# Clearing two mask rows by a transfer instead of two POOL memsets, and folding one small VectorE maximum into the instruction before it, in a streaming attention and recurrence layer

## Chip, cores and metric

The kernel runs on one core of a Trainium2 chip. The metric is the device time of one execution in microseconds (us); the times shown are medians over runs. One execution was also taken with the hardware profiler, and all rows below come from it.

The engines are named as in the profile: PE is TensorE (PEld its weight loads), DVE is VectorE, ACT is ScalarE, POOL is GpSimd, SP is the engine that issues most transfers.

## What is computed

One encoder layer is applied to a prompt of 1024 frames and to 64 frames that continue another stream (256 cached frames). Two branches share one input projection: eight softmax heads of width 64 whose logits carry a cumulative log-forget bias ("FoX"), and four gated linear-recurrence heads ("HGRN2"). Cut to the part that the change touches:

```python
def fox_attend(q, k, v, c_q, c_k, q_pos, k_pos):
    s = jnp.einsum('bqhd,bkhd->bhqk', q, k) * (FOX_HEAD_DIM ** -0.5)
    s = s + (jnp.swapaxes(c_q, 1, 2)[..., :, None] - jnp.swapaxes(c_k, 1, 2)[..., None, :])
    mask = k_pos[None, :] <= q_pos[:, None]
    s = jnp.where(mask, s, -jnp.inf)
    p = jax.nn.softmax(s, axis=-1)
    return jnp.einsum('bhqk,bkhd->bqhd', p, v)
```

The softmax needs, for each query, the maximum of its logits over all earlier keys.

## The kernel before

The kernel first computes the value columns of the prompt (until about 60 us), then the attention (about 60 to 345 us), then the recurrence and the output projection. In the attention the eight heads are taken pair by pair (`PAIRS = (1, 2, 3, 0)`, half `s` 0 and then 1 of each pair). Head n attends while head n+1 is prepared, and projections of later stages (line 234, and 217 for one of them) are laid between as fill work for PE. A generator writes this order by hand, and the tile framework's scheduler then orders the instructions of each engine, by program order and by when it takes operands to be ready; so an edit can also exchange neighbours on an engine.

Per half `s` there is one buffer of each operand: `KX[s]`, `KY[s]` (keys), `QX[s]`, `QY[s]` (queries), all with 128 partitions. In `QY[1]` partitions 64 to 127 hold the queries and partitions 0 to 3 hold rows for the bias and the maximum: rows 0 and 1 are ones, rows 2 and 3 later receive the negated maximum of each query in two parts. The maxima are themselves found by matmuls that read `QY[1]` whole (`Y0[1]` is partitions 0 to 127), so rows 2 and 3 must be zero then, and must be cleared after the head before has used them.

The preparation of a head, in the order of `prepare`:

- `k_prep` copies and splits the keys (ACT line 706, POOL line 711, a transfer at line 710);
- `q_prep` does the same for the queries (ACT line 737, POOL line 743), and for `s = 1` it clears the rows (lines 734 and 735, POOL);
- `max_prep(s, c)` finds the maxima for queries 0 to 511 (`c = 0`) and 512 to 1023 (`c = 1`), four tiles of 128 queries each. PE line 775 makes the logits of one tile in a PSUM bank; for keys on the diagonal piece DVE line 777 adds the mask and takes the maximum in one custom instruction (followed by a small read of its accumulator), and for `c = 1` the earlier 512 keys are first reduced by DVE line 780 into columns 4 to 7 of `mx`. DVE line 783 joins the two;
- `max_columns` makes the two parts of the negated maximum in `mxs` (DVE lines 749 and 750, four columns), and `put_rows` transposes them with four small matmuls (PE line 758) into a PSUM bank, from which ACT line 760 puts them into `QY`;
- `sample_max` does the same for the 64 continued frames (DVE lines 792, 793, 749, 750 with one column, and one more matmul at line 758).

The attention proper is `scores` (PE lines 819 and 820, DVE line 822 for the mask, ACT lines 825 and 826, DVE line 827) and `values` (PE line 844).

Of the kernel before, what the change touches and what calls it, by code (L numbers as in the profile page):

```python
# [13 lines left out]
ALU = mybir.AluOpType  # L14
# [6 lines left out]
T = SEQ + DEC  # L21
# [7 lines left out]
NEG = -3.0e38  # L29
# [32 lines left out]
def f32(ap):  # L62
    return ap.bitcast(F32)
# [3 lines left out]
def tile_fox_hgrn2(  # L67
# [7 lines left out]
    act, dve, pool, pe, sync = nc.scalar, nc.vector, nc.gpsimd, nc.tensor, nc.sync  # L75
# [7 lines left out]
    def nm(s):  # L83
        cnt[0] += 1
        return f"{s}_{cnt[0]}"
# [4 lines left out]
    def bank(tag):  # L90
        return ps.tile([P, 512], F32, tag=tag, name=nm(tag), bufs=PSB[tag])
# [293 lines left out]
    with tc.tile_pool(name="start", bufs=2, side="right") as sp:  # L385
# [132 lines left out]
        def aqt(shape, dt, name):  # L518
            return aq.tile(shape, dt, tag=name, name=name)
# [8 lines left out]
        KY = [aqt([P, KW], F32R, f"KY{s}") for s in range(2)]  # L528
        QY = [aqt([P, T], F32R, f"QY{s}") for s in range(2)]
# [100 lines left out]
    with actx:  # L630
# [66 lines left out]
        def halves(s):  # L697
            return slice(64 * s, 64 * s + 64), slice(64 - 64 * s, 128 - 64 * s)
# [31 lines left out]
        def q_prep(p_, s, c, first):  # L730
            r, o = halves(s)
            qT = qTs[p_]
            if c == 0 and s and p_ != PAIRS[0]:
                pool.memset(f32(QY[s][0:4, :]), 0.0)
                pool.memset(f32(QY[s][0:2, :]), 1.0)
            cs = (slice(0, 512), slice(512, T))[c]
            act.activation(QY[s][r, cs], qT[r, cs], AF.Copy)
            yield 0.0
            if first:
                act.activation(QX[s][o, cs], qT[r, cs], AF.Copy)  # L740
            else:
                sync.dma_start(f32(QX[s][o, cs]), f32(QY[s][r, cs]))
            pool.tensor_tensor(QX[s][r, cs], qT[r, cs], f32(QY[s][r, cs]), op=ALU.subtract)
            yield 0.0

        def max_columns(c, mx, tiles, rows):

            ms = mxs[c]
            dve.tensor_scalar(ms[:rows, :tiles, 2], mx, -1.0, None, op0=ALU.mult)
            dve.scalar_tensor_tensor(ms[:rows, :tiles, 3], mx, -1.0, f32(ms[:rows, :tiles, 2]), op0=ALU.mult,  # L750
                                     op1=ALU.subtract)
# [11 lines left out]
        def max_prep(s, c):  # L763

            qy, ky = QY[s], KY[s]
            rows = Y0[s]
            mx = a2.tile([P, 8], F32, tag="mx", name=nm("mx"))
            for piece in range(c + 1):
                for i in range(4):
                    qs = slice(c * 512 + i * P, c * 512 + (i + 1) * P)  # L770
                    k0 = piece * 512
                    diag = piece == c
                    n = (i + 1) * P if diag else 512
                    pb = bank("tp")
                    pe.matmul(pb[:, :n], qy[rows, qs], ky[rows, k0:k0 + n], start=True, stop=True)  # L775
                    if diag:
                        dve.tensor_tensor_reduce(pb[:, :n], pb[:, :n], cmask[:, 512 - n:512], 1.0,  # L777
                                                 NEG, ALU.add, ALU.max, mx[:, i:i + 1])
                    else:
                        dve.tensor_reduce(mx[:, 4 + i:5 + i], pb[:, :n], axis=AX.X, op=ALU.max)  # L780
                    if diag and i == 3:
                        if c:
                            dve.tensor_tensor(mx[:, 0:4], mx[:, 0:4], mx[:, 4:8], op=ALU.max)
                        max_columns(c, mx[:, 0:4], 4, P)
                    yield max(n / 2.4, 107)

# [10 lines left out]
        def prepare(p_, s, first=False):  # L797

            rest = max_prep(s, 1)
            steps = [k_prep(p_, s, first), q_prep(p_, s, 0, first), max_prep(s, 0), q_prep(p_, s, 1, first), islice(rest, 2),  # L800
                     put_rows(0, s, 4, P), rest, sample_max(s), put_rows(1, s, 4, P), put_rows(2, s, 1, DEC)]
            if first:
                steps[4:6] = steps[5:3:-1]
            steps.insert(1 if first else 8, v_prep(p_, s))
            for g in steps:
                for x in g:
                    yield x
# [690 lines left out]
    for i, rows, src in tok_tiles[:SAMPLE_POS] + tok_tiles[NT:] + tok_tiles[SAMPLE_POS:NT]:  # L1498
# [3 lines left out]
        mx = fin.tile([P, 2, 8, P], F32R, tag="mx", name=nm("mx"))  # L1502
# [102 lines left out]
```

## Time and profile before

| | us |
|---|---|
| median of 3 runs (lowest to highest) | 721.27 (721.17 to 721.51) |
| the profiled execution, its own time | 721.17 |
| its span, first to last instruction | 719.4 |
| PE busy | 702.7 (98% of the span) |
| DVE, ACT, POOL busy | 454.1, 343.5, 192.1 |

A busy PE is the bound on average, but an average hides single stalls; the rows below are read from the stretches where PE stood still. Times in the rows are from the span's start, and the profiled execution took 1.8 us more than its span.

### The profile page before, as it was taken

The page shows a single profiled execution, that of the slowest core. Times are in us where ns is not written, and L with a number is a line of the kernel's source. Part 1 is how long each engine was busy: PE and PEld are TensorE (multiplying, and loading weights), DVE is VectorE, ACT ScalarE, POOL GpSimd, SP SyncE. Part 2 cuts the span into 40 slices and gives each one's busy share as a digit, 9 for nine tenths or more (in the row PEclk, how much of TensorE's full clock was granted, in tenths as well). Part 3 has the DMA queues.
Part 4 walks back from the last instruction along what each step waited for, and adds up shares of the span by engine and source line. Part 5 has one row for each costly group of instructions (what it writes and reads, how often), then busy time and mean ns, then how long its engine had stood idle before and what let it go on. Part 6 is the DMA issues. An engine that isn't in the chain of part 4 may idle for free.

```text
span 719.4 us, 11880 instructions
## 1 busy us (share of the span) xinstructions
PE 702.7 (98%) x4319; PEld 634.7 (88%) x4319; DVE 454.1 (63%) x1145; ACT 343.5 (48%) x877; POOL 192.1 (27%) x252
## 2 busy tenths in 40 slices
PE   9999999999999998999999999999999999999995
PEld 7889989899888897898999999999999998888885
DVE  4445267666777666775536967765795689763541
ACT  6755454657557475867562324224222333323542
POOL 4044932545246234524310001000100100012422
PEclk9999999999999999999999999999999999999999
DMA  8823321221122012110312101002100104331211
GB/s 313 328 84 96 96 99 29 57 81 47 32 92 56 15 28 81 39 30 4 131 44 59 30 31 40 3 30 67 34 31 30 38 34 138 131 111 58 89 44 60
DMA packets 23451, 51.00 MB, mean 71 GB/s; under 512 B 5616, under 2 KB 8512, under 8 KB 23392
## 3 DMA queue, kind: packets, MB, share of 16 engines
q1 hardware_dynamic: 23216, 50.15, 21.8%
q8 instruction: 34, 0.56, 0.3%
q14 instruction: 25, 0.20, 0.1%
q10 hardware_dynamic: 176, 0.09, 0.1%
HBM read 36.32 MB, written 9.56 MB: 64 GB/s over the span
## 4 chain that ended last, share of the span: by engine, by line
PE 87%; DVE 6%; ACT 4%; issue 1%; DMA 0%; POOLq 0%; DVEq 0%; SPq 0%; POOL 0%; ACTq 0%
PE pj L234 36%; PE pj L1384 13%; PE pj L217 6%; PE av L844 6%; PE st L819 2%; PE tp L775 2%; PE st L820 2%; PE pj L440 2%; PE tp L440 2%; PE av L440 2%; PE st L440 2%; PE st L1192 1%; PE st L1271 1%; PE pj L211 1%; PE pj L1378 1%
## 5 line engine op out<-in xcount | busy, mean ns | idle before, releaser
L234 PE MATMUL pj<-hT,whi 128*128 128x364 f32 (+1 forms) x1152 | 213.1, 332 | 0.0
L234 PEld LDWEIGHTS pj<-hT,whi 128*128 128x128 f32 x1152 | 193.3, 189 | 4.6 <-issue 0.3
L234 PE MATMUL pj<-hT,wlo 128*128 128x364 f32 (+1 forms) x576 | 110.0, 331 | 0.0
L234 PEld LDWEIGHTS pj<-hT,wlo 128*128 128x128 f32 x576 | 97.5, 188 | 3.1 <-issue 0.3
L827 DVE TENSOR_TENSOR pl<-st,ph 128x512 fp32r<-128x512 f32 (+1 forms) x96 | 53.1, 556 | 39.2 <-ACT st L826 36.9
L825 ACT ACTIVATE ph<-st 128x512 fp32r<-128x512 f32 (+1 forms) x96 | 46.8, 488 | 60.4 <-DVE st L822 39.1
L107 POOL TENSOR_SCALAR rr<-ss 128x4 f32<-128x4 f32 (+1 forms) x12 | 2.3, 194 | 250.8 <-ACT og L1306 250.6
L1384 PE MATMUL pj<-hT,mx 128*128 128x512 f32 (+1 forms) x264 | 56.3, 374 | 0.0
L1384 PEld LDWEIGHTS pj<-hT,mx 128*128 128x128 f32 x264 | 46.3, 188 | 9.9
L170 ACT ACTIVATE whi<-wr 128x256 fp32r<-128x256 f32 (+1 forms) x112 | 38.6, 407 | 33.8 <-PE pj L234 18.8
L171 POOL TENSOR_TENSOR wlo<-wr,whi 128x256 fp32r<-128x256 f32 (+1 forms) x56 | 39.8, 738 | 39.8 <-ACT whi L170 23.1
L826 ACT ACTIVATE st<-st 128x512 f32<-128x512 f32 (+1 forms) x96 | 46.5, 485 | 0.0
L819 PE MATMUL st<-QX,KX 128*128 128x512 f32 (+1 forms) x96 | 35.5, 370 | 3.4 <-DVE pl L827 3.3
L217 PE MATMUL pj<-whi,hT 128*128 128x264 f32 (+1 forms) x256 | 37.0, 287 | 0.0
L1384 PE MATMUL pj<-hT,mxp 128*128 128x512 f32 x144 | 36.4, 403 | 0.0
L777 DVE CUSTOM_DVE_ANT_0 tp<-tp,cmask 128x128 f32<-128x128 f32 (+1 forms) x64 | 31.1, 501 | 7.3 <-PE tp L775 6.9
L217 PEld LDWEIGHTS pj<-whi,hT 128*128 128x128 f32 x256 | 33.9, 189 | 1.7 <-issue 0.3
L711 POOL TENSOR_TENSOR KX<-kT,KX 64x544 fp32r<-64x544 f32 x16 | 21.6, 1354 | 50.9 <-ACT KX L706 42.3
L844 PE MATMUL av<-ph,VH 128*128 128x512 f32 (+1 forms) x96 | 34.8, 363 | 0.2 <-ACT ph L825 0.2
L820 PE MATMUL st<-QY,KY 68*128 68x512 f32 (+3 forms) x96 | 33.5, 348 | 0.0
L844 PE MATMUL av<-pl,VH 128*128 128x512 f32 (+1 forms) x96 | 33.2, 346 | 0.0
L844 PE MATMUL av<-ph,VL 128*64 128x512 f32 (+1 forms) x96 | 32.4, 338 | 0.0
(311 smaller groups left out, 1358.4 us busy)
## 6 DMA issues: line engine op xcount, KB each, us to landing
wr<-in_w_t_dram SPq DMA_DIRECT2D x24, 512.0 KB
x<-in_xT_dram SPq DMA_DIRECT2D x16, 272.0 KB
xn<-in_x_prompt_dram SPq DMA_DIRECT2D x8, 512.0 KB
wo_raw<-in_w_out_dram SPq DMA_DIRECT2D x8, 512.0 KB
yp<-in_x_prompt_dram SPq DMA_DIRECT2D x6, 512.0 KB
out_dram<-yp SPq DMA_DIRECT2D x12, 256.0 KB
out_dram<-kT SPq DMA_DIRECT2D x4, 544.0 KB
wv<-in_w_v_dram SPq DMA_DIRECT2D x8, 256.0 KB
```

Source lines behind the costliest of these rows:

```text
L170: act.activation(hf[:, cs], raw[:, cs], AF.Copy)
L171: self.eng.tensor_tensor(lf[:, cs], raw[:, cs], f32(hf[:, cs]), op=ALU.subtract)
L217: pe.matmul(pb[:rows, :width], a[:, j, t0:t0 + rows], w[j // 4][b][:, j % 4, :], start=(g == 0 and j == 0), stop=(g == 2 and j == 7))
L234: pe.matmul(pb[:, :n], w[:, j, :], h[:, j, t0:t0 + n], start=(g == 0 and j == 0), stop=(g == 2 and j == 7))
L440: pe.matmul(pb[:, :WV], x[:, j, t0:t0 + P], w[:, j, :], start=(j == 0 and a == 0 and b == 0), stop=(j == 7 and a == 1))
L819: pe.matmul(st[:, :n], kx[:, ks], qx[:, qs], start=True, stop=False)
L820: pe.matmul(st[:, :n], ky[YM[s], ks], qy[YM[s], qs], start=False, stop=True)
L825: act.activation(ph[:, :n], st[:, :n], AF.Exp)
L826: act.activation(st[:, :n], st[:, :n], AF.Exp)
L827: dve.tensor_tensor(pl[:, :n], st[:, :n], f32(ph[:, :n]), op=ALU.subtract)
L844: pe.matmul(av[mm, cols], w[:, b, :], x[:, :n], start=(b == 0 and w is VH[s] and x is ph), stop=(b == nblk - 1 and w is VL[s]), skip_group ...
L1384: pe.matmul(pb[:rows, :n], mx[:, a, j, :rows], wo[b][:, j0 + j, c0:c0 + n], start=(g == 0 and j == 0), stop=(g == 2 and j == nj - 1))
```

## The change

```diff
@@ q_prep
             if c == 0 and s and p_ != PAIRS[0]:
-                pool.memset(f32(QY[s][0:4, :]), 0.0)
-                pool.memset(f32(QY[s][0:2, :]), 1.0)
+
+                sync.dma_start(f32(QY[s][2:4, :]), f32(KY[s][4:6, 0:T]))
@@ max_prep
                     if diag:
                         dve.tensor_tensor_reduce(pb[:, :n], pb[:, :n], cmask[:, 512 - n:512], 1.0,
-                                                 NEG, ALU.add, ALU.max, mx[:, i:i + 1])
+                                                 mx[:, 4 + i:5 + i] if c else NEG, ALU.add, ALU.max,
+                                                 mx[:, i:i + 1])
                     else:
                         dve.tensor_reduce(mx[:, 4 + i:5 + i], pb[:, :n], axis=AX.X, op=ALU.max)
                     if diag and i == 3:
-                        if c:
-                            dve.tensor_tensor(mx[:, 0:4], mx[:, 0:4], mx[:, 4:8], op=ALU.max)
                         max_columns(c, mx[:, 0:4], 4, P)
```

Three times in the program (the preparation of the fourth, sixth and eighth head) two POOL memsets of 4 and 2 partitions x 1088 give way to one transfer of 2 partitions x 1088 on SP's queue, from two partitions of `KY[1]` that hold zeros throughout. Eight times the DVE instruction of line 783 goes, and in exchange 32 of the 64 custom maxima (line 777 with `c = 1`) start from a column of `mx` instead of a constant. In the rows of the changed kernel lines 779 and 780 count one more, and lines from 784 on one less.

The engines' orders differ otherwise in a few places. The first is the end of the seventh head's maxima (in the program: the last rows of `max_prep(0, 1)` and `sample_max(0)` of pair 0). On DVE there stood before (names with numbers are single buffers; `mxs_547` is the four-column result, `mxs_548` the one-column result):

```order
L827 TENSOR_TENSOR pl_3244<-st_3239,ph_3243 128x256
L783 TENSOR_TENSOR mx_3105<-mx_3105 128x4
L792 TENSOR_TENSOR tp_3277<-tp_3277,cmask 64x64
L749 TENSOR_SCALAR mxs_547<-mx_3105 128x4
L822 TENSOR_TENSOR st_3283<-st_3283,kmask 128x128
L750 SCALAR_TENSOR_TENSOR mxs_547<-mx_3105,mxs_547 128x4
L793 TENSOR_REDUCE mx_3276<-tp_3277 64x1
L822 TENSOR_TENSOR st_3298<-st_3298,kmask 128x128
L749 TENSOR_SCALAR mxs_548<-mx_3276 64x1
L750 SCALAR_TENSOR_TENSOR mxs_548<-mx_3276,mxs_548 64x1
```

and now, on the same engine and at the same place:

```order
L826 TENSOR_TENSOR pl_3236<-st_3231,ph_3235 128x256
L749 TENSOR_SCALAR mxs_547<-mx_3097 128x4
L791 TENSOR_TENSOR tp_3268<-tp_3268,cmask 64x64
L750 SCALAR_TENSOR_TENSOR mxs_547<-mx_3097,mxs_547 128x4
L821 TENSOR_TENSOR st_3274<-st_3274,kmask 128x128
L792 TENSOR_REDUCE mx_3267<-tp_3268 64x1
L821 TENSOR_TENSOR st_3289<-st_3289,kmask 128x128
L749 TENSOR_SCALAR mxs_548<-mx_3267 64x1
L750 SCALAR_TENSOR_TENSOR mxs_548<-mx_3267,mxs_548 64x1
```

Line 783 is gone, and one mask (822, now 821) has moved from between lines 749 and 750 to behind them. On POOL at that place the eighth head's preparation and a weight split (line 171) stood before as:

```order
L171 TENSOR_TENSOR wlo_3265<-wr_2559,whi_3264 128x256 x4
L727 TENSOR_TENSOR VL_680<-vnat_91,VH_544 128x512
L734 MEMSET QY_543 4x1088
L711 TENSOR_TENSOR KX_677<-kT_1988,KX_677 64x544
L735 MEMSET QY_543 2x1088
L171 TENSOR_TENSOR wlo_3372<-wr_3274,whi_3371 128x256
```

and now:

```order
L171 TENSOR_TENSOR wlo_3256<-wr_2553,whi_3255 128x256 x4
L727 TENSOR_TENSOR VL_680<-vnat_91,VH_544 128x512
L711 TENSOR_TENSOR KX_677<-kT_1984,KX_677 64x544
L171 TENSOR_TENSOR wlo_3362<-wr_3265,whi_3361 128x256
L852 TENSOR_TENSOR mixF_2505<-mixF_2505,rd_3329 64x512
```

The key split of line 711 now follows line 727 directly. On PE the same place read before:

```order
L844 MATMUL av_3101<-ph_3243,VH_545 128x256
L234 MATMUL pj_3362<-hT,whi_3264 128x364
L819 MATMUL st_3298<-QX_678,KX_676 128x512
L820 MATMUL st_3298<-QY_542,KY_540 128x512
L844 MATMUL av_3101<-pl_3244,VH_545 128x256
L758 MATMUL tp_3311<-ident,mxs_547 4x128 x4
L844 MATMUL av_3101<-ph_3243,VL_681 64x256
L758 MATMUL tp_3320<-ident,mxs_548 4x64
L234 MATMUL pj_3362<-hT,whi_3264 128x364 x6
```

and now:

```order
L843 MATMUL av_3093<-ph_3235,VH_545 128x256
L234 MATMUL pj_3352<-hT,whi_3255 128x364 x2
L818 MATMUL st_3289<-QX_678,KX_676 128x512
L819 MATMUL st_3289<-QY_542,KY_540 128x512
L758 MATMUL tp_3302<-ident,mxs_547 4x128 x4
L843 MATMUL av_3093<-pl_3236,VH_545 128x256
L843 MATMUL av_3093<-ph_3235,VL_681 64x256
L758 MATMUL tp_3311<-ident,mxs_548 4x64
L234 MATMUL pj_3352<-hT,whi_3255 128x364 x5
```

One projection matmul (234) has moved ahead of the four transposing matmuls of line 758, and one of line 844 behind them. The second place is the end of the first head's maxima. DVE there read before:

```order
L777 ISA tp_1038,mx_980<-tp_1038,cmask 128x512
L777 ISA mx_980 128x1
L792 TENSOR_TENSOR tp_1057<-tp_1057,cmask 64x64
L783 TENSOR_TENSOR mx_980<-mx_980 128x4
L822 TENSOR_TENSOR st_1069<-st_1069,kmask 128x128
L749 TENSOR_SCALAR mxs_547<-mx_980 128x4
L793 TENSOR_REDUCE mx_1056<-tp_1057 64x1
L750 SCALAR_TENSOR_TENSOR mxs_547<-mx_980,mxs_547 128x4
L827 TENSOR_TENSOR pl_1074<-st_1069,ph_1073 128x128
L749 TENSOR_SCALAR mxs_548<-mx_1056 64x1
L750 SCALAR_TENSOR_TENSOR mxs_548<-mx_1056,mxs_548 64x1
```

and now:

```order
L777 ISA tp_1038,mx_980<-tp_1038,cmask,mx_980 128x512
L777 ISA mx_980 128x1
L791 TENSOR_TENSOR tp_1056<-tp_1056,cmask 64x64
L826 TENSOR_TENSOR pl_1034<-st_1029,ph_1033 128x256
L749 TENSOR_SCALAR mxs_547<-mx_980 128x4
L792 TENSOR_REDUCE mx_1055<-tp_1056 64x1
L750 SCALAR_TENSOR_TENSOR mxs_547<-mx_980,mxs_547 128x4
L821 TENSOR_TENSOR st_1068<-st_1068,kmask 128x128
L749 TENSOR_SCALAR mxs_548<-mx_1055 64x1
L750 SCALAR_TENSOR_TENSOR mxs_548<-mx_1055,mxs_548 64x1
L826 TENSOR_TENSOR pl_1073<-st_1068,ph_1072 128x128
```

The one-column results (749 and 750 into `mxs_548`) now stand ahead of the subtraction (827, now 826) that they stood behind.

## Rows read from the trace of the kernel before

**Rows 1.** The profile's page: busy time, share of the span and number of instructions of two engines, and the chain that ended last by engine.
```profile
PE 702.7 (98%) x4319; PEld 634.7 (88%) x4319; DVE 454.1 (63%) x1145; ACT 343.5 (48%) x877; POOL 192.1 (27%) x252
PE 87%; DVE 6%; ACT 4%; issue 1%; DMA 0%; POOLq 0%; DVEq 0%; SPq 0%; POOL 0%; ACTq 0%
```

**Rows 2.** PE's own waits over the whole span: who waited for whom, us in total, times, longest.
```profile
PE st L819 <- DVE pl L827: 3.3, 5, 1.0
PE tp L758 <- DVE mxs L750: 3.3, 3, 2.4
```

**Rows 3.** Busy time by stretch, PE alone. Columns: stretch, its length, PE busy us (instructions), granted clock (1.00 is 2.4 GHz), busy share of the DMA engines, GB/s.
```profile
282.10:285.50 3.40, 0.65 (x7) 1.00 0.56 196
285.50:288.92 3.42, 3.42 (x15) 0.58 0.00 0
288.92:292.33 3.41, 3.41 (x21) 0.92 0.00 0
```

**Rows 4.** Timeline of PE around 284 us. Columns, here and in the timelines below: start us, us, engine, line, operation, out<-in, form, count, and in brackets the idle time before it and what ended it.
```profile
281.82 0.28 PE L844 MATMUL av<-pl,VH 128*128 128x256 f32 x1
284.52 0.40 PE L758 MATMUL tp<-ident,mxs 128*4 128x128 f32 x4 [2.42 <-DVE mxs L750]
...
285.37 0.19 PE L758 MATMUL tp<-ident,mxs 64*4 64x64 f32 x1 [0.33 <-DVE mxs L750]
...
285.49 1.73 PE L234 MATMUL pj<-hT,whi 128*128 128x364 f32 x6
...
294.15 1.50 PE L234 MATMUL pj<-hT,whi 128*128 128x364 f32 x8
```

**Rows 5.** Timeline of DVE in the same stretch.
```profile
281.11 1.01 DVE L783 TENSOR_TENSOR mx<-mx 128x4 f32<-128x4 f32 x1
...
282.18 0.89 DVE L749 TENSOR_SCALAR mxs<-mx 128x4 fp32r<-128x4 f32 x1
282.24 1.01 DVE L822 TENSOR_TENSOR st<-st,kmask 128x128 f32<-128x128 f32 x1
283.17 1.29 DVE L750 SCALAR_TENSOR_TENSOR mxs<-mx,mxs 128x4 fp32r<-128x4 f32 x1
284.39 0.47 DVE L793 TENSOR_REDUCE mx<-tp 64x1 f32<-64x320 f32 x1
284.79 0.28 DVE L822 TENSOR_TENSOR st<-st,kmask 128x128 f32<-128x128 f32 x1
...
285.16 0.15 DVE L750 SCALAR_TENSOR_TENSOR mxs<-mx,mxs 64x1 fp32r<-64x1 f32 x1
```

**Rows 6.** Timeline of POOL in the same stretch; POOL's next instruction after these is at 290.87.
```profile
280.80 1.29 POOL L727 TENSOR_TENSOR VL<-vnat,VH 128x512 fp32r<-128x512 f32 x1
282.05 0.99 POOL L734 MEMSET QY<- 4x1088 f32 x1
283.12 1.32 POOL L711 TENSOR_TENSOR KX<-kT,KX 64x544 fp32r<-64x544 f32 x1
284.38 0.99 POOL L735 MEMSET QY<- 2x1088 f32 x1
```

**Rows 7.** Timeline of DVE in the preparation of the fourth head: the same instructions, first with POOL idle and then, at 188.86, with POOL's line 711 running from 188.62 to 189.97.
```profile
187.13 0.15 DVE L783 TENSOR_TENSOR mx<-mx 128x4 f32<-128x4 f32 x1
187.32 0.17 DVE L749 TENSOR_SCALAR mxs<-mx 128x4 fp32r<-128x4 f32 x1
187.53 0.17 DVE L750 SCALAR_TENSOR_TENSOR mxs<-mx,mxs 128x4 fp32r<-128x4 f32 x1
...
188.86 1.12 DVE L750 SCALAR_TENSOR_TENSOR mxs<-mx,mxs 64x1 fp32r<-64x1 f32 x1
```

**Rows 8.** Groups of DVE instructions by form: count | busy us, mean ns of one | idle before. Line 974 scales a PSUM tile by one value per partition, line 822 adds two tiles.
```profile
L822 DVE TENSOR_TENSOR st<-st,kmask 128x128 f32<-128x128 f32 x64 | 19.8, 310 | 8.4 <-PE st L820 8.3
L974 DVE TENSOR_SCALAR hi<-pj,rn 128x128 f32<-128x128 f32 x16 | 5.5, 344 | 7.1 <-ACT hi L973 6.9
L777 DVE CUSTOM_DVE_ANT_0 tp<-tp,cmask 128x128 f32<-128x128 f32 x16 | 4.7, 293 | 1.9 <-PE tp L775 1.9
```

**Rows 9.** Timelines of DVE and PE at the end of the first head's maxima.
```profile
99.56 0.29 DVE L827 TENSOR_TENSOR pl<-st,ph 128x128 fp32r<-128x128 f32 x1 [0.56 <-ACT st L826]
...
99.93 0.15 DVE L750 SCALAR_TENSOR_TENSOR mxs<-mx,mxs 64x1 fp32r<-64x1 f32 x1
...
100.14 0.19 PE L758 MATMUL tp<-ident,mxs 64*4 64x64 f32 x1 [0.51 <-DVE mxs L750]
```

**Rows 10.** Timelines of DVE, POOL and PE at the end of the second head's maxima.
```profile
124.54 1.01 DVE L750 SCALAR_TENSOR_TENSOR mxs<-mx,mxs 128x4 fp32r<-128x4 f32 x1
...
124.17 1.36 POOL L711 TENSOR_TENSOR KX<-kT,KX 64x544 fp32r<-64x544 f32 x1 [4.41 <-ACT KX L706]
...
129.53 0.39 PE L819 MATMUL st<-QX,KX 128*128 128x256 f32 x1 [1.04 <-DVE pl L827]
```

**Rows 11.** Timelines of ACT, SP and PE: the copy that line 711 waits for, the weight transfer issued just ahead of where the new transfer is to stand, and the first matmuls that read the cleared rows.
```profile
280.70 0.66 ACT L706 ACTIVATE KX<-kT 64x544 fp32r<-64x544 f32 x1
...
280.87 0.35 SPq L160 DMA_DIRECT2D wr<-in_w_t_dram  x1
...
289.22 0.52 PE L775 MATMUL tp<-KY,QY 128*128 128x128 f32 x2
```

**Rows 12.** Timeline of PE in the preparation of the sixth head, at full clock, a little behind that head's transposes.
```profile
224.70 0.39 PE L819 MATMUL st<-QX,KX 128*128 128x256 f32 x1 [0.75 <-DVE pl L827]
```

## Prediction

> **What bounds the kernel.** I read the page first: PE is busy 98% of the span and carries 87% of the chain that ended last [rows 1]. An edit that takes work from DVE and POOL (63% and 27% busy) can therefore give back only time in which PE stood still or ran slowly. Next come PE's own waits, which are short [rows 2]: the longest two kinds are 3.3 us each, and the one that the change touches is line 758 (the transposes of the maxima) waiting for line 750. Of its 3.3 us, 2.4 are a single wait. So I went to that wait, in the timelines around 284 us.
>
> There PE finishes the subtraction part of line 844 at 282.1 and starts line 758 only at 284.52; 0.33 us more are lost before the one-column transpose at 285.37 [rows 4]. In the stretch 282.10 to 285.50 PE is busy 0.65 of 3.40 us, and behind it the granted clock is 0.58 and then 0.92 of full, which between two levels (1.00 for 2.4 GHz, 0.5 for 1.2 GHz) means some 3.4 us at 1.2 GHz [rows 3]. So the stall costs twice: 2.75 us of standing still, and after it (1 - 0.58) x 3.42 + (1 - 0.92) x 3.41 = 1.7 us of lost clock.
>
> Why was line 750 late? DVE's three small instructions 783, 749 and 750 took 1.01, 0.89 and 1.29 us [rows 5], where the same ones take 0.15, 0.17 and 0.17 with POOL idle [rows 7]. Each ended within 0.04 us of the end of a POOL instruction: 783 at 282.12 (POOL's 727 ends at 282.09), 749 at 283.07 (the memset 734 ends at 283.04), 750 at 284.46 (711 ends at 284.44) [rows 5, 6]. The same happens at 188.86, where line 750 runs to 189.98 and POOL's 711 to 189.97 [rows 7]. So one DVE instruction was held behind one POOL instruction, three times in turn, and the change takes away one of each: 783 on DVE and 734 on POOL.
>
> **The rule behind it.** These rows show small SBUF-to-SBUF instructions of DVE waiting out a whole POOL instruction. The Trainium skill's page "SBUF — State Buffer" (SBUF: two separate sides) says the same: VectorE and GpSimd arbitrate for a port pair, "an exclusive lock, not a bandwidth split", held for the whole instruction by whichever starts first. The trace agrees with the holding. What would follow if DVE were the one to start first is the third case below.
>
> **Term 1, the stall at 284 us.** Without the memset, line 711 follows 727 at 282.09; its operand is ready, since line 706 ends at 281.36 [rows 6, 11]. It takes 1.32 us, to 283.41. Line 749 now stands where 783 stood, is held by 727 and ends at 282.12; line 750 comes behind it and is held by 711, to 283.44. Line 758 followed 750's end by 0.06 us, so it starts at 283.50 instead of 284.52. From 750's end to the one-column transpose passed 0.91 us (284.46 to 285.37); now one more mask lies in it (line 822, 0.28 us long, of which I count 0.20 since DVE's instructions overlap a little [rows 5]), so that transpose starts at 283.44 + 0.91 + 0.20 = 284.55, 0.82 us earlier than 285.37. One projection matmul now lies ahead of the wait instead of behind it: about 0.17 us (1.50 us for eight with a last end of some 0.33, [rows 4]). Together 1.0 us. Bounds: 0 if 750 is held as long as before by something else, 1.8 us in the third case.
>
> **Term 2, the clock.** What PE stands still there shrinks from 2.75 to about 1.9 us, in two pieces (to 283.50, then about 0.55 us). Does the clock still fall? The rows that bound it: the stall of 2.42 and 0.33 us was followed by a fall [rows 3, 4]; the one of 1.04 us at 129.53 was not, nor 0.75 at 224.70 [rows 10, 12] (the only stretch at low clock inside the kernel's work is the one of rows 3). The new value lies between. I take "no fall" as likelier, because the idle time is cut by a third and broken up. The gain is then at most 1.7 us; at full clock ACT and DVE have less time ahead of PE, and at the sibling place PE waits 0.75 us for line 827 [rows 12], so at least 0.95. I take 1.5.
>
> **Term 3, the first head.** There the one-column transpose waits 0.51 us for line 750, which stands behind a subtraction (827) that itself waits 0.56 us for ACT [rows 9]. The new order puts 749 and 750 ahead of that subtraction. I take 0.4 us, bounds 0.5 gained and 0.3 lost (the order also moves one mask of line 822 behind other work there, and ACT's exponentials with it, by about that).
>
> **Term 4, the second head.** With 783 gone and 750 moved ahead of the reduction 793, line 750 is due about 0.4 us earlier than 124.54, that is at about 124.15. POOL's 711, which held it for 1.01 us, starts at 124.17 [rows 10]. Who is first is open. If 750 is, the DVE work behind it moves up by some 0.7 us, and of the 1.04 us that PE waits at 129.53 up to 0.4 goes. I take 0, with 0.4 as bound.
>
> **Term 5, the new operand.** 32 maxima now read a start value per partition. The trace has no such form of line 777; the nearest rows: a PSUM tile of 128x128 scaled by one value per partition takes 344 ns, two tiles added take 310, and the maximum itself 293 [rows 8]. So 0 to 51 ns each, 0 to 1.6 us over DVE in all, against 8 x 0.15 us that line 783 gave (the held one apart). Nearly all of it lies beside PE's projections; I charge PE 0.1 us, bounds 0 and 0.3.
>
> **Term 6, the memsets and the transfer.** Six memsets of 1.0 us leave POOL. Apart from the one at 282.05 nothing of PE waited for them, so this counts 0. Each new transfer moves two partitions of 4.4 KB and waits for the same readers as the memset did. On SP the third one stands behind the weight transfer at 280.87 and ahead of the key copy [rows 11], which it can delay by one issue, some 0.4 us; that copy is needed only for the second half of the keys. The transfers that were under way there had all ended by 285.50, since the DMA engines' share is 0.00 from then on [rows 3]. The first matmul that reads the cleared rows stood at 289.22 [rows 11] and comes, with terms 1 and 2, at about 286.6. So I cost the transfer at 0, covered by 1.1 us of other PE work at the worst place.
>
> **Sum**, against the profiled execution's own 721.17 us (its span of 719.4 and 1.8 around it; the median of the runs is 721.27, 0.10 more): 721.17 - 1.0 - 1.5 - 0.4 + 0.1 = 718.4 us. 0.2% (1.44 us) is about what a measurement of this kernel can tell from no change.
>
> **The rivals.**
> - *The clock still falls.* Half a microsecond to a microsecond less standing still may not be enough; 1.9 us is nearer to 2.75 than to 1.04. Then term 2 is gone: 719.9 us, range 719.4 to 720.5, on the edge of what can be told.
> - *Line 750 goes first.* POOL holds DVE here because it started first each time; if line 750 starts ahead of 711, POOL waits for it instead. The rule of the Trainium skill's page "SBUF — State Buffer" (above) allows both. Against it: between 283.07 and 283.17 POOL's next instruction was in before 750 [rows 5, 6]. Then line 758 starts near 282.4, the one-column 750 is held by 711 instead (as at 188.86), and term 1 is 1.8 us: 717.6 us, down to 717.1 with term 4.
> - *Nothing moves.* Another POOL instruction takes the place of the memset, and DVE is held as long; only terms 3 and 5 remain: about 720.9 us.
> - *Slower: the transfer lands late.* A memset was in POOL's own order; a transfer has to be issued behind the weight load, run and report. From 286.6 us on, each microsecond that it lands later stops PE for one, and a stop like that of rows 4 brings the clock down as well (1.7 us). It takes a landing near 288.8 for the kernel to be even with before, and near 290 for slower by 0.2%. At the other two places the readers come 5 us and more after the issue. Price: 722.7 us or more. The idle DMA engines after 285.50 speak against it.
>
> **How the numbers follow.** My sum (no fall of the clock) 0.56, the clock still falls 0.25, line 750 first 0.07, nothing moves 0.06, the late transfer 0.06. The likeliest alone: 717.7 to 719.3. The range from 717.2 to 720.6 takes in the second and third cases and leaves out the last two. Faster by over 0.2% (below 719.83): 0.56 + 0.07 + a quarter of the second case = 0.70; within 0.2%: 0.24; slower: 0.06.
>
> **What would show it.** In the changed kernel: 727 and 711 back to back on POOL near 281 to 283.5; 749 and then 750 ending with them; line 758's longest wait about 1.3 us instead of 2.42; a granted clock of 1.00 behind it; no 0.51 us wait at the first head; line 777 at 0 to 51 ns more with `c = 1`; the first line 775 with the cleared rows not waiting. The prediction is wrong if the clock stays low behind a stall of under 2 us, if DVE meets another POOL instruction there, or if line 775 waits for the transfer.

## The result and the profile after

The changed kernel takes 716.97 us (median of 6 runs, 716.74 to 717.40) where the kernel before, on the same chip, takes 721.32 (721.00 to 721.51): a ratio of 0.9941, 95% interval 0.9931 to 0.9951. That is 4.35 us gained; the prediction said 2.8 us, and 716.97 lies 0.2 us below its range. On a second chip the two took 717.15 and 721.54 us (0.9936, interval 0.9924 to 0.9948). The traced execution took 717.02 us, its span 715.3.

Names of lines: in the changed kernel 749, 750, 758, 711 and 727 keep their numbers, the transfer is line 735, and 822, 827, 792, 793, 819, 820 and 844 are now 821, 826, 791, 792, 818, 819 and 843.

First the page's busy times, which answer the first line of [rows 1]:

```profile
PE 701.2 (98%) x4319; PEld 632.6 (88%) x4319; DVE 453.2 (63%) x1137; ACT 343.4 (48%) x877; POOL 186.7 (26%) x246
```

PE has the same number of instructions and is busy 1.5 us less; DVE gives up the eight instructions of line 783, POOL the six memsets. Next PE's waits (who waited for whom, us in total, times, longest), which answer [rows 2]:

```profile
PE st L818 <- DVE pl L826: 3.5, 6, 1.0
...
PE tp L758 <- DVE mxs L750: 0.8, 2, 0.5
```

Line 758's wait for line 750 has gone from 3.3 us in all and 2.4 in one piece to 0.8 and 0.5. The other kind is unchanged but for one new wait of 0.17 us. The timelines of DVE, POOL, PE and SP at the seventh head, which answer [rows 4 to 6]:

```profile
280.22 1.29 POOL L727 TENSOR_TENSOR VL<-vnat,VH 128x512 fp32r<-128x512 f32 x1
...
280.64 0.90 DVE L749 TENSOR_SCALAR mxs<-mx 128x4 fp32r<-128x4 f32 x1
280.73 0.64 SPq L735 DMA_DIRECT2D QY<-KY  x1
...
281.46 0.21 DVE L791 TENSOR_TENSOR tp<-tp,cmask 64x64 f32<-64x64 f32 x1
...
281.59 0.16 DVE L750 SCALAR_TENSOR_TENSOR mxs<-mx,mxs 128x4 fp32r<-128x4 f32 x1
281.59 1.35 POOL L711 TENSOR_TENSOR KX<-kT,KX 64x544 fp32r<-64x544 f32 x1
...
281.80 0.40 PE L758 MATMUL tp<-ident,mxs 128*4 128x128 f32 x4 [0.28 <-DVE mxs L750]
...
282.46 0.14 DVE L749 TENSOR_SCALAR mxs<-mx 64x1 fp32r<-64x1 f32 x1
282.63 0.33 DVE L750 SCALAR_TENSOR_TENSOR mxs<-mx,mxs 64x1 fp32r<-64x1 f32 x1
...
283.02 0.19 PE L758 MATMUL tp<-ident,mxs 64*4 64x64 f32 x1 [0.53 <-DVE mxs L750]
...
285.28 0.39 PE L775 MATMUL tp<-KY,QY 128*128 128x128 f32 x2
```

Line 749 is held by POOL's 727 to 281.54, as was forecast. Line 750 then gets in together with 711 and takes 0.16 us: it is not held. The four transposes start at 281.80 after a wait of 0.28 us in place of 2.42. The one-column 750 is held too, but only for what is left of 711 (which ends at 282.94): it takes 0.33 us, and PE waits 0.53 us there. The transfer is issued at 280.73, and the first matmul that reads its rows (line 775, [rows 11]) stands at 285.28 without a wait. PE's stretches there (length, PE busy, granted clock, busy share of the DMA engines, GB/s), which answer [rows 3]:

```profile
282.00:285.50 3.50, 2.97 (x22) 1.00 0.44 165
285.50:289.00 3.50, 3.33 (x20) 1.00 0.00 0
```

The granted clock stays at 1.00. PE's waits at this place have gone from 2.75 us to 0.81, and the low clock behind them is gone.

**Where the 4.14 us of the two spans lie.** The same matmuls of line 844 (843) can be found in both traces, and the time between two of them compared:

| stretch of PE's work | before | after | difference |
|---|---|---|---|
| start to the first of line 844 | 95.18 | 95.05 | -0.13 |
| to the 7th (end of the first head's maxima) | 6.24 | 5.81 | -0.43 |
| to the 206th | 178.19 | 178.18 | -0.01 |
| to the 232nd (the seventh head's stretch) | 22.34 | 19.43 | -2.91 |
| to PE's last matmul | 410.14 | 410.12 | -0.02 |
| from there to the end of the span | 7.32 | 6.69 | -0.63 |

The first difference is scatter of the start (94.9 to 95.7 us in eleven traces). The last one was in no term of the prediction; it is taken up with the last experiment. The remaining places that the prediction spoke of, in the same order. First head, PE, to [rows 9]:

```profile
99.19 0.52 PE L758 MATMUL tp<-ident,mxs 128*4 128x128 f32 x5
```

The five transposes of line 758 now follow one another without a wait; the 0.51 us is gone. Second head, DVE, POOL and PE, to [rows 10]:

```profile
123.56 0.16 DVE L750 SCALAR_TENSOR_TENSOR mxs<-mx,mxs 128x4 fp32r<-128x4 f32 x1
123.60 1.36 POOL L711 TENSOR_TENSOR KX<-kT,KX 64x544 fp32r<-64x544 f32 x1 [4.41 <-ACT KX L706]
...
128.95 0.38 PE L818 MATMUL st<-QX,KX 128*128 128x256 f32 x1 [1.03 <-DVE pl L826]
```

There too line 750 is now first (0.16 us, 0.04 ahead of 711), and yet PE's wait for line 826 is 1.03 us, as before. Last the groups of line 777 by form (count | busy, mean ns of one | idle before), to [rows 8]; the one that names `mx` among its operands reads the start value:

```profile
L777 DVE CUSTOM_DVE_ANT_0 tp<-tp,cmask,mx 128x128 f32<-128x128 f32 x8 | 2.8, 349 | 0.0
...
L777 DVE CUSTOM_DVE_ANT_0 tp<-tp,cmask 128x128 f32<-128x128 f32 x8 | 2.4, 294 | 1.6 <-PE tp L775 1.6
```

The start value costs 55 ns at 128 columns, 61 at 256 (492 against 431), 57 at 384 (624 against 567) and 26 at 512 (750 against 724).

### The profile page after: what moved, and what is told of

Read it like the earlier page. It is cut to its first block, busy times and chain, and to the rows that moved or that the text cites. A ratio compares the mean times of both kernels' runs of the same rounds, so it can differ in the third digit from the quotient of the medians.

```text
span 715.3 us, 11877 instructions
## 1 busy us (share of the span) xinstructions
PE 701.2 (98%) x4319; PEld 632.6 (88%) x4319; DVE 453.2 (63%) x1137; ACT 343.4 (48%) x877; POOL 186.7 (26%) x246
## 4 chain that ended last, share of the span: by engine, by line
PE 89%; DVE 4%; ACT 4%; issue 1%; DMA 0%; POOLq 0%; DVEq 0%; SPq 0%; POOL 0%; ACTq 0%
PE pj L234 38%; PE pj L1383 13%; PE pj L217 6%; PE av L843 6%; PE st L818 2%; PE tp L775 2%; PE st L819 2%; PE pj L440 2%; PE tp L440 2%; PE av L440 2%; PE st L440 2%; PE st L1191 1%; PE st L1270 1%; PE pj L211 1%; PE pj L1377 1%
## 5 line engine op out<-in xcount | busy, mean ns | idle before, releaser
L1383 PEld LDWEIGHTS pj<-hT,mxp 128*128 128x128 f32 x144 | 26.3, 188 | 6.2 <-issue 0.3
```

Of the source, the lines that this page charges most:

```text
L1383: pe.matmul(pb[:rows, :n], mx[:, a, j, :rows], wo[b][:, j0 + j, c0:c0 + n], start=(g == 0 and j == 0), stop=(g == 2 and j == nj - 1))
```

## Experiments

Two facts set the plan. The scheduler's order on DVE, PE and ACT depends on the fold alone: with the fold it is that of the changed kernel, without it that of before, whichever way the rows are cleared (the traces below have these orders). So transfer and memsets can be exchanged without moving anything on those engines. And the stretch from the 206th to the 232nd matmul of line 844 holds 106 matmuls in each kernel, so its length compares them without the scatter of the start. The table collects what the experiments below gave. The stall is PE's waits for line 750 at the seventh head; stall, clock and stretch are those of the one traced execution, and the chip's own median of before stands beside each median.

| kernel | median us (before) | ratio, 95% interval | stall, us | clock behind it | stretch, us |
|---|---|---|---|---|---|
| before | 721.32 | 1 | 2.42 + 0.33 | 0.5 for 3.41 us | 22.34 |
| before, again | 721.62 (721.54) | 1.0004, 0.9995 to 1.0014 | 2.42 + 0.32 | 0.5 for 3.41 us | 21.94 |
| changed | 716.97 (721.32) | 0.9941, 0.9931 to 0.9951 | 0.28 + 0.53 | 1.00 | 19.43 |
| changed, again | 717.15 (721.54) | 0.9936, 0.9924 to 0.9948 | 0.28 + 0.53 | 1.00 | 19.44 |
| transfer alone | 719.18 (721.68) | 0.9971, 0.9960 to 0.9982 | 1.50 + 0.32 | 0.5 for 3.41 us | 21.49 |
| fold alone | 718.26 (721.68) | 0.9955, 0.9941 to 0.9968 | 1.22 + 0.53 | 0.5 for 3.41 us | 21.12 |
| changed, POOL's time back | 717.70 (721.68) | 0.9945, 0.9932 to 0.9957 | 0.27 + 0.34 | 1.00 | 19.24 |
| changed, line 750 later | 718.17 (721.68) | 0.9955, 0.9942 to 0.9967 | 1.38 + 0.33 | 1.00 | 20.25 |
| changed, first head unfolded | 717.38 (721.54) | 0.9943, 0.9931 to 0.9956 | 0.27 + 0.53 | 1.00 | 19.42 |
| stall put back | 720.18 (721.54) | 0.9973, 0.9957 to 0.9989 | 2.32 + 0.29 | 0.5 for 6.83 us | 22.58 |
| before, fetch moved | 720.37 (721.55) | 0.9981, 0.9972 to 0.9990 | 2.42 + 0.32 | 1.00 | 21.31 |

**The transfer alone.** The kernel before, with

```diff
-                pool.memset(f32(QY[s][0:4, :]), 0.0)
-                pool.memset(f32(QY[s][0:2, :]), 1.0)
+                sync.dma_start(f32(QY[s][2:4, :]), f32(KY[s][4:6, 0:T]))
```

Expected:

> The kernel before with the transfer in place of the six memsets, and line 783 kept; the order on DVE, PE and ACT is that of before. Theory (which of DVE's small instructions stands behind which POOL instruction decides): line 783 is still held by POOL's 727 to about 282.1 us, 749 goes next, and 750 is held by 711, which now follows 727 directly, to about 283.5. Line 758's longest wait falls from 2.42 to about 1.5 us, so 1.0 us is gained (the first term of the prediction as it was worked out), and 1.7 more if the clock no longer falls: 718.6 us without a fall, 720.3 with one. The first head's 0.51 us wait stays. Rival (what counts is that POOL loses the memsets, however DVE is ordered): 717.0, as with the whole change. Rival (the fold did it all): 721.3.

Measured: 719.18 against 721.68 us. Timelines of DVE, POOL and PE:

```profile
280.94 1.01 DVE L783 TENSOR_TENSOR mx<-mx 128x4 f32<-128x4 f32 x1
...
282.01 0.15 DVE L749 TENSOR_SCALAR mxs<-mx 128x4 fp32r<-128x4 f32 x1
282.01 1.34 POOL L711 TENSOR_TENSOR KX<-kT,KX 64x544 fp32r<-64x544 f32 x1
...
282.28 1.10 DVE L750 SCALAR_TENSOR_TENSOR mxs<-mx,mxs 128x4 fp32r<-128x4 f32 x1
...
283.43 0.41 PE L758 MATMUL tp<-ident,mxs 128*4 128x128 f32 x4 [1.50 <-DVE mxs L750]
```

This is the course that the prediction's first term described, in another kernel: 727 holds the first small instruction (783), the second (749) slips in beside 711, and the third (750), which has a mask of 0.28 us ahead of it here, finds 711 running and is held to 283.38. The wait is 1.50 us. In this execution the clock fell:

```profile
284.90:288.30 3.40, 3.40 (x14) 0.50 0.03 8
```

It did not in all: four of its seven executions have a mean granted clock of 0.996 or less, as this one (each trace with a low clock behind the stall has 0.996 or less, each without one 0.997), and take 719.18 to 721.57 us; the other three have 0.997 or 0.998 and take 718.62 to 718.98. The theory of the holds is borne out, and so is the prediction's rival that a stall of this size may still bring the clock down. The times came near the forecast partly by luck: the traced span is 1.9 us shorter than that of before, of which 0.85 lie in the stretch and 0.9 in the tail, which the expectation did not count (the last experiment takes it up). Neither edit did it all.

**The fold alone.** The changed kernel, with the two memsets in place of the transfer. Expected:

> The changed kernel with the six memsets back in place of the transfers; the order on DVE, PE and ACT is that of the changed kernel. Theory: at the seventh head 749 is held by 727, to about 281.5 us; the memset 734 is then in on POOL. Of the rows of before and after, no memset held a two-input instruction (line 750 at 285.16 took 0.15 us inside the memset at 284.38), so 750 goes through and line 758 starts near 281.8 with a wait of 0.3; line 711 runs one memset later, to about 283.9, and holds the one-column 750 until then, so the second wait is 1.4 in place of 0.53 us. That is 0.9 us more than the whole change: 717.9 if the clock holds, 719.6 if it falls. If a memset does hold 750: line 758 starts at 282.5, and about 718.2. Rival (the fold brings only the first head's wait): 720.7.

Measured: 718.26 against 721.68 us. DVE, POOL and PE:

```profile
280.20 1.30 POOL L727 TENSOR_TENSOR VL<-vnat,VH 128x512 fp32r<-128x512 f32 x1
...
280.63 1.83 DVE L749 TENSOR_SCALAR mxs<-mx 128x4 fp32r<-128x4 f32 x1
...
281.44 0.99 POOL L734 MEMSET QY<- 4x1088 f32 x1
...
282.50 0.17 DVE L750 SCALAR_TENSOR_TENSOR mxs<-mx,mxs 128x4 fp32r<-128x4 f32 x1
282.51 1.36 POOL L711 TENSOR_TENSOR KX<-kT,KX 64x544 fp32r<-64x544 f32 x1
...
282.72 0.40 PE L758 MATMUL tp<-ident,mxs 128*4 128x128 f32 x4 [1.22 <-DVE mxs L750]
```

That is the theory's 717.9 and the 0.36 us by which before is slower on this chip; but the number agrees by luck, as the course is another one. Here 749 is passed over twice, by 727 and then by the memset, which started at 281.44, 0.06 us before 727 had ended. It ends at 282.46, and then 750 is in ahead of 711. So the tie between a waiting DVE instruction and POOL's next one went to POOL here. The traced execution, with the low clock, took 718.73 us; three of the five have a mean granted clock of 0.997 and take 717.90 to 718.26.

**The whole change, with POOL's time back.**

```diff
                 sync.dma_start(f32(QY[s][2:4, :]), f32(KY[s][4:6, 0:T]))
+                pool.memset(f32(KY[s][32:36, 0:T]), 0.0)
+                pool.memset(f32(KY[s][32:34, 0:T]), 0.0)
```

Expected:

> The whole change, and beside each transfer two POOL memsets of zeros, as long as the old ones, over rows of KY that hold zeros throughout: POOL has its old work back and nothing else changes. Theory (POOL's order against DVE's, not the transfer): the same as the fold alone, 717.9 if the clock holds and 719.6 if it falls, with the same waits within 0.2 us. Rival (the transfer itself gains or costs something on the way of PE): it differs from the fold alone by over 0.5 us. Rival (POOL's time does not matter once line 783 is gone): 717.0.

Measured: 717.70 against 721.68 us, 4.0 us faster than before, nearly all of the change. Its rows (lines from 736 on count one more, so 751 is 750 and 759 is 758):

```profile
281.68 1.00 POOL L735 MEMSET KY<- 4x1088 f32 x1
281.69 0.16 DVE L751 SCALAR_TENSOR_TENSOR mxs<-mx,mxs 128x4 fp32r<-128x4 f32 x1
...
281.91 0.41 PE L759 MATMUL tp<-ident,mxs 128*4 128x128 f32 x4 [0.27 <-DVE mxs L751]
...
282.74 0.15 DVE L751 SCALAR_TENSOR_TENSOR mxs<-mx,mxs 64x1 fp32r<-64x1 f32 x1
```

The expectation was wrong here, and usefully so. This memset starts 0.06 us after 727, not before its end; 749 was free by then, and 750 runs through the memset without being held. The memset now stands between 727 and 711 as a shield: 711 starts only at 282.75, so that the one-column 750 at 282.74 is in ahead of it and not held either, and the stretch is the shortest of all, 19.24 us. The memsets' time on POOL was not the cost; where 711 stands against 750 was. The median is 0.56 us under that of the fold alone, the size that the first rival had named for the transfer; the traces show another reason for it, the memset's start 0.06 us after instead of before the end of 727, though no run moved that start alone. (In this trace PE also waited 0.7 us near 613 us for ACT's line 1371, which no other trace shows.)

**The whole change, with line 750 later.** At the seventh head line 749 of the four columns is issued twice (the scheduler then also puts one mask, line 821, ahead of line 750 again, and one matmul of line 843 ahead of the transposes):

```diff
-            dve.tensor_scalar(ms[:rows, :tiles, 2], mx, -1.0, None, op0=ALU.mult)
+            for _ in range(2 if twice else 1):
+                dve.tensor_scalar(ms[:rows, :tiles, 2], mx, -1.0, None, op0=ALU.mult)
```

Expected:

> The whole change, with line 749 of the seventh head's four columns issued twice, so that line 750 comes one small instruction and one mask later and POOL's 711 is first. This is the course that the prediction took. Theory: the second 749 takes the place in which 750 slipped in ahead of 711; 750 is held to about 283.0 us, line 758 starts there with a wait of 1.1 to 1.2 in place of 0.28, and PE loses 0.8 to 1.0 us against the whole change: 717.9 us if the clock holds (then the size of this stall, 1.6 to 1.8 us in two pieces, does not bring the clock down), 719.6 if it falls. Rival (who is first on the port is worth nothing): 717.0.

Measured: 718.17 against 721.68 us, so 3.5 us gained where the whole change gains 4.4. DVE, POOL and PE (lines one more, 750 is 749):

```profile
281.82 0.16 DVE L750 TENSOR_SCALAR mxs<-mx 128x4 fp32r<-128x4 f32 x1
281.82 1.34 POOL L711 TENSOR_TENSOR KX<-kT,KX 64x544 fp32r<-64x544 f32 x1
...
282.09 1.10 DVE L751 SCALAR_TENSOR_TENSOR mxs<-mx,mxs 128x4 fp32r<-128x4 f32 x1
...
283.25 0.40 PE L759 MATMUL tp<-ident,mxs 128*4 128x128 f32 x4 [1.38 <-DVE mxs L751]
```

As expected: the second 749 takes the place in which 750 had slipped in, 750 is held by 711 to 283.19, and PE waits 1.38 us, about as the prediction had it (1.3). The stretch grows by 0.82 us against the changed kernel, the stall by 0.90. The clock stayed up in this execution behind a stall of 1.71 us, and by the mean granted clock (0.997 or more) in two others; the remaining two have 0.995 and 0.996 and take 719.50 and 718.47 us:

```profile
284.90:288.30 3.40, 3.23 (x21) 1.00 0.00 0
```

**The stall put back.** The fold alone, with line 749 issued twice as above. Expected:

> The fold, with the memsets kept and line 749 of the seventh head's four columns issued twice. Theory (the holds alone make the stall): 749 is held by 727 and the memset to 282.5 us, the second 749 goes ahead of 711, 750 is held by 711 to about 283.9, and line 758 waits 2.4 us as before, although line 783 is gone. The clock falls in nearly every execution. The time is that of before less the first head's 0.5: 720.6 to 720.9 where before takes 721.3, 3.6 to 3.9 us slower than the change. Rival (the change gained by something else than the stall): 718 or less.

Measured: 720.18 against 721.54 us. DVE, POOL and PE:

```profile
281.42 1.02 POOL L734 MEMSET QY<- 4x1088 f32 x1
...
281.55 0.92 DVE L750 TENSOR_SCALAR mxs<-mx 128x4 fp32r<-128x4 f32 x1
...
282.52 1.32 POOL L711 TENSOR_TENSOR KX<-kT,KX 64x544 fp32r<-64x544 f32 x1
282.58 1.29 DVE L751 SCALAR_TENSOR_TENSOR mxs<-mx,mxs 128x4 fp32r<-128x4 f32 x1
...
283.93 0.40 PE L759 MATMUL tp<-ident,mxs 128*4 128x128 f32 x4 [2.32 <-DVE mxs L751]
```

PE alone behind it (length, PE busy, granted clock, busy share of the DMA engines, GB/s):

```profile
284.30:291.10 6.80, 6.50 (x24) 0.50 0.00 1
```

With line 783 gone and one small instruction set in its place, the three holds of before are back one for one (750 is held by 711, which starts at 282.52), and with them 2.32 us of waiting and, in nine of eleven executions, the low clock (0.996 or less). This kernel is 3.0 us slower than the changed one on the same chip, where 3.6 to 3.9 were expected. The gain left over before is 1.36 us, more than expected: 0.43 at the first head, and a tail shorter by 0.7 (below), which the expectation did not count. So the stall with its clock is what the change gained in the middle, and neither the work that DVE no longer does nor the work that POOL no longer does.

**The first head alone.** The changed kernel, with the constant and line 783 kept at the first head. Expected:

> The changed kernel, with the constant as start value and line 783 kept at the first head alone: there the order of DVE is that of before again. Theory (the third term is the order of the one-column results at the first head): PE's wait of 0.51 us for line 750 near 100 us is back and nothing else moves: 0.4 to 0.6 us slower than the change, 717.5 where the change takes 717.0. Rival (the small gain in front of 101 us comes from the fold's cheaper DVE work): no wait, and within 0.2 us of the change.

Measured: 717.38 us where the changed kernel took 717.15 on the same chip; in the traces the stretch to the 7th matmul is 6.24 us, as before, and 5.81 with the change. DVE and PE:

```profile
99.72 0.15 DVE L750 SCALAR_TENSOR_TENSOR mxs<-mx,mxs 64x1 fp32r<-64x1 f32 x1
...
99.93 0.19 PE L758 MATMUL tp<-ident,mxs 64*4 64x64 f32 x1 [0.51 <-DVE mxs L750]
```

The one-column 750 stands behind the subtraction again, at 99.72 instead of 99.23, and the 0.51 us wait of PE is back. The third term is this order, at 0.43 us by the traces; the medians differ by 0.23, less than the 0.4 that was expected at the least.

**The kernel before and the changed one, again.** Expected:

> The kernel before once more, for its trace. In the first trace the last transfer had its last packet 2.58 us after the issue, in the five other traces so far 1.91 us; an instruction fetch of 8 KB stood at 715.93 to 716.62 us on the DMA engines, in the middle of it. Theory: where the program fetches its instructions is fixed, so the 2.58 comes again and 0.7 to 0.9 us of what the change gained lie in the tail and not in its mechanism. Rival: chance of one execution; then the tail is 1.91 here, and the span near 718.6. The stall at 284 us is again 2.75 us and the clock falls behind it, in either case.

> The changed kernel once more, beside the kernel before and the two below on one chip. Theory: faster than before by 4.0 to 4.5 us again; PE's stall at the seventh head 0.8 us in two pieces, and no low clock inside the work in any execution.

Measured: see the table. Both traces repeat the first ones, but for 0.40 us in the stretch of before (21.94 for 22.34). The long tail of before comes again too, so it was not the chance of one execution. Here is the end of before (second trace), all engines (PE, PEld, DVE, ACT, POOL, then the granted clock, the busy share of the DMA engines, GB/s), and one DMA queue in the first of the two stretches (packets, MB, share of 16 engines):

```profile
715.94:717.40 1.46, 0.00 (x0) 0.00 (x0) 0.00 (x0) 0.00 (x0) 0.00 (x0) 0.94 0.95 353
717.40:718.15 0.75, 0.00 (x0) 0.00 (x0) 0.00 (x0) 0.00 (x0) 0.00 (x0) 0.50 0.06 24
```

```profile
q14 instruction: 1, 0.01, 2.9%
```

Behind the bulk of the last transfer 0.06 of the DMA engines, that is one of 16, stays busy for another 0.7 us, and in the bulk stands one packet of instructions (8 KB of the program itself, which the DMA engines bring in beside the data: an instruction fetch), which takes 0.69 us on one engine, from 716.15 on. The same two stretches of the changed kernel:

```profile
712.50:713.96 1.46, 0.00 (x0) 0.00 (x0) 0.00 (x0) 0.00 (x0) 0.00 (x0) 0.50 0.96 358
713.96:714.71 0.75, 0.00 (x0) 0.00 (x0) 0.00 (x0) 0.00 (x0) 0.00 (x0) 0.50 0.00 0
```

**The kernel before, with the fetch moved.** Four small instructions more, early in the program:

```diff
         dve.tensor_tensor(lbe[:], lbe[:], lbr[:], op=ALU.mult)
+        spare = pool_.tile([P, 8], F32, tag="spare", name="spare", bufs=1)
+        for z in range(3):
+            act.activation(spare[:, z:z + 1], hgv[:, z:z + 1], AF.Copy)
+        sync.dma_start(spare[:, 4:8], hg_vecs[:, 0:4])
```

Expected:

> The kernel before with both memsets and line 783, and four small instructions more at about 58 us, which nothing reads: three copies of one column on ACT and one transfer of 128x4 on SP. All other instructions and their order are those of before. Theory (both traces of before have an 8 KB instruction fetch in the middle of the last transfer, none of the other kernels has; where it falls is a matter of how many instructions stand ahead of it): the fetch moves out of the last transfer, whose last packet comes 1.9 us after the issue in place of 2.57, and the kernel is 0.6 to 0.9 us faster than before, 720.6 to 720.9 where before takes 721.5, with the stall of 2.75 us and the low clock at 284 us as in before. Rival (the fetch is not what delays the packet, or these two engines' fetches are others): the same tail as before, and the same time within 0.3 us.

Measured: 720.37 against 721.55 us: 1.2 us faster, for adding instructions, and 0.3 more than expected. PE at the seventh head (758 is 762 here), then two stretches behind that and the stretch behind the bulk of the last transfer, columns as above:

```profile
284.86 0.40 PE L762 MATMUL tp<-ident,mxs 128*4 128x128 f32 x4 [2.42 <-DVE mxs L754]
```

```profile
284.20:287.60 3.40, 2.42 (x17) 2.17 (x18) 1.62 (x6) 1.77 (x4) 1.52 (x2) 1.00 0.27 93
287.60:291.00 3.40, 3.21 (x21) 2.79 (x20) 3.06 (x10) 2.75 (x6) 0.73 (x1) 1.00 0.00 0
...
716.50:717.25 0.75, 0.00 (x0) 0.00 (x0) 0.00 (x0) 0.00 (x0) 0.00 (x0) 0.50 0.00 0
```

The end of the last transfer is that of the changed kernel: the fetch has moved to 712.91, ahead of the last transfer, and its last packet comes 1.91 us after the issue in place of 2.57. Between PE's last matmul and the end, the changed kernel gains 0.67 us by this and 0.25 behind the last packet, and loses 0.29 because ACT's line 1523 (now 1522) starts that much later behind DVE (2.58 us idle before it in place of 2.29); it does so in the five traces of kernels with both the transfer and the fold and in none of the others, for a reason that stays open. So it owes some 0.65 us of its 4.35 to where an instruction fetch falls. What puts the fetch there was not taken further; that four instructions on ACT and SP move it was shown. The rows show a second thing that was not expected: with the stall of before unchanged, the granted clock stays at 1.00 in this execution, which took 719.80 us. That does not account for the median: ten of the twelve executions have a mean granted clock of 0.996 or less, and their median of 720.5 is still 1.0 us under before. Of that the shorter tail gives 0.8 in the trace (7.32 to 6.54 us); the rest stays open.

## Why the prediction missed

- **What bounds the kernel, and the holds:** right. The stall was three holds in a row; taking one link from each engine undid it, and putting one instruction back (stall put back) restored it.
- **Term 1, the stall: the step that failed.** It said "line 750 comes behind it and is held by 711, to 283.44". In the changed kernel 750 came in beside 711 and was not held (timeline above, against [rows 6]). Before and after differ here by 1.88 us (21.31 in before with the fetch moved, where the clock also stayed up, less 19.43), not by 1.0. The judgement that POOL's next instruction would be first was drawn from 283.07 to 283.17 [rows 5], where a mask of line 822 stands between 749 and 750. The new order, which the section on the change shows, has only line 792 (now 791) there, and that had begun while 749 was still held. With a mask between, 750 does lose (transfer alone, line 750 later); with 791 alone between, it was in at once, in both traces of the changed kernel and in the one with the first head unfolded. The rival "line 750 goes first" was therefore the case to forecast, and not one of 0.07; its 1.8 us were right (1.88).
- **Term 2, the clock:** no fall was right, but by luck, and 1.5 us was too much. It stayed up behind 0.81 us, the stall that was left because term 1 had failed; behind stalls near the forecast 1.9 us it fell in four of seven executions (1.82 us, transfer alone) and in two of five (1.71 us, line 750 later). Behind the same stall the stretch takes 22.34 and 21.94 us with the low clock and 21.31 without: 0.6 to 1.0 us. The term counted half of 3.42 us. Matmul by matmul against that kernel, PE falls behind by up to 1.48 us in the first trace of before and 1.12 in the second, and part of it comes back because waits of 0.18 and 0.35 us behind the stall vanish when PE is late (at 288.70 and 292.69 in before with the fetch moved; the first trace of before has only the second of them, its second trace neither). The reason given, that the stall becomes shorter than a bound between 1.04 and 2.75 us, is too simple: between these sizes both happen. In the traces the clock fell behind 1.50 + 0.32 and 1.22 + 0.53, and did not behind 1.38 + 0.33, nor once behind 2.42 + 0.32. At 0.81 us and less none of 21 executions shows one (mean granted clock 0.997 or more).
- **Term 3, the first head:** 0.43 us in the traces for 0.4, shown by undoing it.
- **Term 4, the second head:** 0, as chosen. The condition of its bound came true (750 first) and gave PE nothing: line 826, for which PE waits, stands behind ACT's exponentials and not behind DVE's order.
- **Terms 5 and 6:** 26 to 61 ns for the start value, against 0 to 51 (over the bound at three of four widths), and nothing of it on PE: the table's two stretches without a stall differ by 0.02 us or less, where 0.1 was charged. The transfer cost nothing, with 4.5 us between its issue and its first reader.
- **No term:** 0.63 us in the tail. The prediction's sum put everything behind 345 us at nothing without saying so.

Sum by the traces: -1.88 (stall) - 1.03 (clock) - 0.43 - 0.63 - 0.13 (start) - 0.03 = -4.13 us, for 4.14 between the spans. The sum of the prediction missed 0.9 us in term 1 and 0.6 in the tail, and had 0.5 too much in term 2; with the stall right and all else as it was, it would have given 717.5, inside its range.

Of the rivals, "the clock still falls" did not come in the changed kernel but does in some executions of the transfer alone; "nothing moves" and "slower" are out: line 775 never waited.

## What to carry to other kernels

Where a small VectorE instruction waits for a GpSimd one, list both engines' orders side by side and ask, pair by pair, which stands *directly* behind the one that holds; one small instruction and a mask of 0.3 us ahead of line 750 decided 0.8 us of the stretch here. Work that an engine gives up is worth nothing by itself; in this kernel POOL could have all its memset time back at no loss in the stretch once it fell in another place. And a gain of half a microsecond in a program of this length can be the place of an instruction fetch: compare the tail behind the last matmul before crediting an edit with it.

## What the runs showed of the hardware

- **Which POOL instruction holds which DVE instruction.** Line 750, two inputs in SBUF, is held by POOL's subtractions (1.10 and 1.29 us in the rows above) but takes 0.16 us inside a memset (POOL's time back, 281.69). Line 749 with four columns, one input, is held by a memset too (0.92 us in the kernel with the stall put back), while with one column it takes 0.14 us in the middle of 711 (282.46 in the changed kernel). The Trainium skill's page "SBUF — State Buffer" (SBUF: two separate sides) says of the shared ports that a DVE instruction with two SBUF inputs contends "only against a GpSimd op that reads SBUF"; the rows of line 750 agree.
- **Who wins a tie.** The DVE instruction next behind the freed one (line 791 or 792 aside) started within 0.01 us of POOL's next subtraction and was not held in each trace where the two met (changed kernel, transfer alone, line 750 later, first head unfolded; behind the memset also the fold alone). With a mask in between, 750 was held in each (before, transfer alone, line 750 later, stall put back). Against a memset, which starts 0.06 us before 727 ends, it went both ways: 749 was passed over and took 1.83 us in the fold alone, and was freed after 0.89 us where the stall was put back.
- **The clock.** The same stall of 2.42 and 0.32 us is followed by 3.41 us at 1.2 GHz in two traces and by none in a third. How long PE stood still is thus not all that decides; what else does is open.
- **Instruction fetch.** An 8 KB fetch in the middle of a transfer kept one of the 16 DMA engines 0.7 us longer, and with it the end of the kernel.
